# Two-layer hybrid encoder on one core: first loads in wider rows, whole conditioning sums, and group A's queries prepared by head pairs

## The chip, the cores and the metric

The kernel runs on one core of a Trainium2 chip. The metric is device time in microseconds (us), the median of several executions. The engines are named as in the profile: PE (TensorE matmul; PEld is its weight load), DVE (VectorE), ACT (ScalarE), POOL (GpSimd) and SP (SyncE, which issues the DMAs here).

## What is computed

One batch of 1024 tokens of width 1024 goes through two layers and a final RMSNorm, all in float32.

```
mod = silu(c) @ ada_w[layer] + ada_b[layer]; shift, scale, gate = split(mod, 3)
h = rms_norm(x, norm_w[layer]) * (1 + scale) + shift
layer 0: qa, ka, va, ga, cq, ckv, kr, gb = split(h @ w_in)
         A: qa, ka = axial_rope(rms_norm(qa)), axial_rope(rms_norm(ka))   # 8 heads of 64, 2 key heads
            oa = softmax(qa ka^T / 8) va * silu(ga)
         B: latent attention from cq, ckv, kr (8 heads), * silu(gb)
         y = concat(oa, ob) @ w_out
layer 1: windowed attention with 16 heads, * silu(gate), @ w_out
x = x + gate * y        (each layer);   out = rms_norm(x)
```

The change touches three things in layer 0: the shift and scale sums of the conditioning, the normalisation of the first 512 tokens, and the per-head normalisation and rotation of group A's queries and keys.

## The kernel before

The engine calls of the program aren't issued where they stand. A `Recorder` (whose one emitting line, L483, is the line of nearly all rows of the profile) collects every operation with its dependences, a priority (its place in the program, plus a shift) and a cost, runs a list schedule over the engines, PSUM banks and SBUF buffers, and then writes out a fixed order for each engine. The function `cost` prices a two-input operation on POOL at 147 ns plus 2.11 ns for each element of a partition. On the chip each engine works through its own list in order and waits at an instruction whose operands aren't there. So a change in a function moves instructions on all engines, and the place that an instruction got in the list holds also where its operands come later than planned.

Matrix products are split into high and low parts: a factor is rounded to fp32r (`h`), the rest is kept (`l`), and three products (`mm3`) make one exact one. The stages that matter here:

- **Start.** `xT_half(0)` loads x of the first 512 tokens, transposed, in eight chunks `kc` of 128 features, squares them on ACT, adds them on DVE, and `rstd_rows` turns the sums into 1/rms (transposes on PE, two reductions on DVE, a power on POOL, four transposes on PE). `warm` puts idle transposes into PE's list here, 14 of them and then 20. DVE multiplies all eight chunks by 1/rms. Then for each `kc`: `ada_mods` makes the scale and shift column (a weighted row sum of 1024 columns each, `ada_sum`, in two parts of 512 columns, and one addition), ACT applies them twice (`modulate`, way "normed": the fp32r `hT00h` and the float32 value), DVE subtracts (`hT00l`), and PE takes that chunk into the products `c1` (keys, values and latents) and `c3` (queries) of four token tiles: 24 matmuls for each chunk.
- **The rest of the projections.** `c2` (compressed queries) of the first half, the same for the second 512 tokens (`hT01`), then `c1`, `c3` and `c2` of its four tiles.
- **Keys and queries of group A.** The keys of all 1024 tokens lie in `karaw`; they are normalised and rotated by key head, and then transposed and split into `khh` (ACT) and `kll` (DVE), which every score product of group A reads. The queries are handled by token tile in `q_rope_a(i)`: all eight heads of 128 tokens at once, eight times; ACT squares, DVE reduces, POOL makes the power, DVE multiplies, POOL and DVE rotate, POOL adds. Each tile is written to `q_sp` in HBM. `q_stack_a(p)` later loads the two heads of pair p for all tokens (pair 0 comes from SBUF), transposes them on PE and splits them into `Qa`.
- **Attention of group A.** 16 groups (head, half of the queries). For each of four query tiles `softmax_unit` makes scores on PE, a maximum on DVE, an exponential on ACT (`Pa`), a reciprocal on DVE, and POOL scales `Pa`. `pv_step` transposes the four on PE, splits them (`hla`) and multiplies with the values `VA`. Between them `gate_fill` puts the matmuls of the gates (`wg0`, `wg4`, ...).

Of the kernel before, what the change touches and what calls it, by code (L numbers as in the profile page):

```python
# [505 lines left out]
def encoder_kernel(ctx: ExitStack, tc: tile.TileContext, xt, ada_t, w_c1, w_c2, w_c3, w_g0, w_uq, w_ukv, w_out0, w_v1,  # L506
# [130 lines left out]
    def ada_sum(o, src, scale, first, name, mark, parts):  # L637

        s = U(name)
        load(s, src, mark)  # L640
        n = 1024 // parts
# [5 lines left out]
    def ada_mods(l, kc, mark=None):  # L647

        t = SM(f"ada{l}{kc}")
        k = 8 * l + kc  # L650
        for j in range(2):
            o = [t[:, 2 * q + j:2 * q + j + 1] for q in range(2)]
            scale, first = (0.5, cols[:, C_BSH + k:C_BSH + k + 1]) if j else (nwh[:, k:k + 1], a0[:, k:k + 1])
            ada_sum(o, ada_t[l * 24 + 8 * (1 - j) + kc], scale, first, f"ada{l}{kc}{j}", mark, 2)
        nc.vector.tensor_tensor(out=mods[:, 2 * k:2 * k + 2], in0=t[:, 0:2], in1=t[:, 2:4], op=ALU.add)

    def ada_gate(l, b, mark=None):
        for t in range(4 * b, 4 * b + 4):
            k = 8 * l + t
            ada_sum([gcol[:, k:k + 1]], ada_t[l * 24 + 16 + t], 0.25, g0[:, k:k + 1], f"adag{l}{t}", mark, 1)  # L660
# [17 lines left out]
    def rstd_rows(accs, name):  # L678
# [20 lines left out]
        nc.gpsimd.tensor_tensor(out=r[:, 0:nt], in0=v, in1=mhalf[:, 0:nt], op=ALU.pow)  # L699
# [70 lines left out]
    xT = {}  # L770

# [29 lines left out]
    marks = {}  # L801
# [24 lines left out]
    qz = [U(f"qz{j}").rearrange("p (t c) -> p t c", t=2) for j in range(4)]  # L826
# [11 lines left out]
    def c3_end(i):  # L838
        nc.scalar.copy(qz[i // 2][:, i % 2, :], c3[i])
# [35 lines left out]
    with issue_after(m_):  # L875
        for i in range(E3, 4):
            c3_part(i, w3, range(KC))
            c3_end(i)
        for i in range(C2_EARLY):
            c2_tile(i)  # L880
    for i in range(E1, NT):
        c1_part(i, w1, range(KC))
        c1_end(i)
# [959 lines left out]
```

## Time and profile before

| | us |
|---|---|
| median of 3 runs | 1205.65 (1204.23 to 1207.63) |
| the profiled execution, its own time | 1205.73 |
| its span, first to last instruction | 1204.0 |
| PE busy | 1168.4 (97%) |
| PEld busy | 986.9 (82%) |
| DVE busy | 920.2 (76%) |
| ACT busy | 658.4 (55%) |
| POOL busy | 557.0 (46%) |

The profiled execution stands 0.08 us above the median. Its span leaves 1.73 us of its own time outside. Busy shares are means over the whole span; rows of the trace give the start of an instruction in us from the span's start and then its length. A bracket at a row's end is the time for which the engine stood idle before it, and what it waited for.

### The profile page before, as it was taken

The page shows a single profiled execution, that of the slowest core. Times are in us where ns is not written, and L with a number is a line of the kernel's source. Part 1 is how long each engine was busy: PE and PEld are TensorE (multiplying, and loading weights), DVE is VectorE, ACT ScalarE, POOL GpSimd, SP SyncE. Part 2 cuts the span into 40 slices and gives each one's busy share as a digit, 9 for nine tenths or more (in the row PEclk, how much of TensorE's full clock was granted, in tenths as well). Part 3 has the DMA queues.
Part 4 walks back from the last instruction along what each step waited for, and adds up shares of the span by engine and source line. Part 5 has one row for each costly group of instructions (what it writes and reads, how often), then busy time and mean ns, then how long its engine had stood idle before and what let it go on. Part 6 is the DMA issues. An engine that isn't in the chain of part 4 may idle for free.

```text
span 1204.0 us, 17922 instructions
## 1 busy us (share of the span) xinstructions
PE 1168.4 (97%) x6320; PEld 986.9 (82%) x6320; DVE 920.2 (76%) x1787; ACT 658.4 (55%) x1346; POOL 557.0 (46%) x551
## 2 busy tenths in 40 slices
PE   6999899999999999999999999999999999999996
PEld 6898778787778878788878888988888888888896
DVE  7976587878687988888798995749886697788343
ACT  4643256666665777787787312228755556653212
POOL 0057765435564655444447233305465265467321
PEclk9999899999999999999999999999999999999999
DMA  9601123120121121001025584200011121045112
GB/s 351 258 1 58 37 103 123 36 105 19 50 95 53 59 82 54 22 15 45 8 73 217 202 314 142 86 1 13 25 53 54 52 88 54 19 180 189 69 71 71
DMA packets 37338, 106.72 MB, mean 89 GB/s; under 512 B 3840, under 2 KB 9472, under 8 KB 37248
## 3 DMA queue, kind: packets, MB, share of 16 engines
q1 hardware_dynamic: 36480, 103.48, 23.9%
q0 software_dynamic: 768, 2.10, 0.7%
q8 instruction: 49, 0.80, 0.3%
q14 instruction: 41, 0.34, 0.1%
HBM read 82.36 MB, written 23.20 MB: 88 GB/s over the span
## 4 chain that ended last, share of the span: by engine, by line
PE 83%; DVE 9%; ACT 4%; issue 2%; DMA 1%; POOL 0%; SPq 0%; POOLq 0%; DVEq 0%; ACTq 0%
PE psum L483 83%; DVE nm L483 2%; DVE hla L483 1%; DVE p L483 1%; ACT q L483 1%; ACT k L483 1%; DVE Qa L483 1%; DMA ada<-in_ada_t 1%; ACT Pa L483 0%; DVE ada L483 0%; DVE q L483 0%; ACT p L483 0%; DVE hl L483 0%; ACT hlb L483 0%; DVE hlb L483 0%
## 5 line engine op out<-in xcount | busy, mean ns | idle before, releaser
L483 DVE TENSOR_REDUCE nm<-psum 128x1 f32<-128x1024 f32 x128 | 155.4, 1217 | 19.0 <-PE psum L483 17.4
L483 POOL TENSOR_SCALAR p<-p,dn 128x384 f32<-128x384 f32 (+1 forms) x128 | 74.1, 597 | 160.3 <-DVE dn L483 79.3
L483 DVE TENSOR_TENSOR hla<-psum,hla 128x512 fp32r<-128x512 f32 x128 | 84.9, 682 | 25.0 <-ACT hla L483 24.4
L483 PE MATMUL psum<-hla,VA 128*128 128x512 f32 x256 | 94.4, 421 | 5.4 <-DVE hla L483 4.0
L483 ACT CAST hla<-psum 128x512 fp32r<-128x512 f32 x128 | 72.4, 592 | 43.4 <-PE psum L483 36.4
L483 PE MATMUL psum<-ident,Pa 128*128 128x128 f32 x512 | 93.8, 272 | 0.8 <-DVE q L483 0.8
L483 POOL TENSOR_SCALAR Pb<-Pb,rs 128x1024 f32<-128x1024 f32 x64 | 71.8, 1125 | 45.6 <-DVE rs L483 43.9
L483 PE MATMUL psum<-hlb,VB 128*128 128x512 f32 x256 | 90.8, 427 | 2.1 <-DVE hlb L483 1.4
L483 POOL TENSOR_SCALAR Pa<-Pa,rs 128x1024 f32<-128x1024 f32 x64 | 76.5, 1198 | 34.7 <-DVE rs L483 32.0
L483 ACT ACTIVATE Pa<-psum,nm 128x1024 f32<-128x1024 f32 x64 | 71.5, 1118 | 32.1 <-DVE nm L483 24.6
L483 DVE TENSOR_TENSOR hlb<-psum,hlb 128x512 fp32r<-128x512 f32 x128 | 82.3, 683 | 7.7 <-ACT hlb L483 7.0
L483 ACT ACTIVATE Pb<-psum,nm 128x1024 f32<-128x1024 f32 x64 | 71.8, 1123 | 25.2 <-DVE nm L483 22.2
L483 PE MATMUL psum<-k,q 128*128 128x512 f32 x256 | 84.1, 400 | 0.2 <-ACT Pb L483 0.2
L483 DVE CUSTOM_DVE_ANT_0 p<-psum,bias,rows_g 128x384 f32<-128x384 f32 (+1 forms) x128 | 70.5, 579 | 12.7 <-PE psum L483 11.5
L483 PE MATMUL psum<-ident,Pb 128*128 128x128 f32 x512 | 79.4, 272 | 0.0
L483 ACT ACTIVATE p<-p,nm 128x384 f32<-128x384 f32 (+1 forms) x128 | 74.1, 585 | 7.1 <-DVE nm L483 7.1
L483 PEld LDWEIGHTS psum<-ident,Pa 128*128 128x128 f32 x512 | 65.0, 140 | 12.4 <-DVE q L483 1.0
L483 ACT CAST hlb<-psum 128x512 fp32r<-128x512 f32 x128 | 68.9, 602 | 9.1 <-PE psum L483 7.8
L483 ACT COPY ot<-psum 64x512 f32<-64x512 f32 x64 | 37.4, 584 | 65.8 <-PE psum L483 65.3
L483 PEld LDWEIGHTS psum<-ident,Pb 128*128 128x128 f32 x512 | 63.2, 140 | 11.3
L483 POOL TENSOR_TENSOR sq<-sq,sq 128x256 f32<-128x256 f32 (+2 forms) x22 | 26.2, 1190 | 76.8 <-ACT sq L483 76.6
L483 PE MATMUL psum<-oTl,wo1h 128*128 128x256 f32 (+1 forms) x192 | 61.2, 320 | 0.0
(748 smaller groups left out, 3653.3 us busy)
## 6 DMA issues: line engine op xcount, KB each, us to landing
ada<-in_ada_t SPq DMA_DIRECT2D x32, 512.0 KB, 8.3
adag<-in_ada_t SPq DMA_DIRECT2D x16, 512.0 KB, 4.8
o<-spill SPq DMA_DIRECT2D x12, 512.0 KB, 6.6
wo0s<-in_w_out SPq DMA_DIRECT2D x8, 512.0 KB, 8.7
xr<-in_xt SPq DMA_DIRECT2D x8, 512.0 KB, 10.0
x_sp<-xr SPq DMA_DIRECT2D x8, 512.0 KB, 3.0
wo1s<-in_w_out SPq DMA_DIRECT2D x8, 512.0 KB, 5.6
x1r<-x_sp SPq DMA_DIRECT2D x8, 512.0 KB, 5.3
```

Of the source, the lines that this page charges most:

```text
L483: fn(*[real(v) for v in a], **{k: real(v) for k, v in kw.items()})
```

## The change

- The first 512 tokens are loaded in four DMAs of 128 x 1024 (4 KB for each partition) in place of eight of 128 x 512.
- `ada_sum` makes one sum of 1024 columns and writes it into `mods` directly; the two halves and their addition go. The sums of layer 0 are ordered behind the power of `rstd_rows`.
- The multiplication by 1/rms is made chunk by chunk, in the loop that uses the chunk. The first reads PSUM, the others a copy in SBUF that ACT makes once.
- `c3_end` copies the four head pairs of a tile into four buffers `qz[p]` (128 tokens x 128 columns each), so ACT makes four copies of 128 columns in place of one of 512.
- `norm_rope_a` replaces the key code and `q_rope_a`. It handles one pair (or the keys) for one half of the tokens. Keys and pair 0 of the first half come right after the first half's projections, the second half after `c3`. Pairs 1 to 3 are written to `q_sp` raw and are normalised and rotated when `q_stack_a` has loaded them, in the attention of group A, with `eng` = POOL for what DVE did.

```
-    def ada_sum(o, src, scale, first, name, mark, parts):
+    def ada_sum(o, src, scale, first, name, mark, late=None):
-        for q in range(parts):
-            c = slice(q * n, (q + 1) * n)
-            nc.vector.tensor_tensor_reduce(out=s[:, c], in0=s[:, c], in1=cb[:, c], scale=scale,
-                                           scalar=0.0 if q else first, op0=ALU.mult, op1=ALU.add, accum_out=o[q])
+        behind(nc.vector.tensor_tensor_reduce(out=s, in0=s, in1=cb, scale=scale, scalar=first, op0=ALU.mult,
+                                              op1=ALU.add, accum_out=o), late)
...
-            for kc in range(KC):
-                load(chunk(xT[0], kc), xt[0, kc // 2][:, (kc % 2) * 512:(kc % 2 + 1) * 512])
+            for k2 in range(4):
+                load(xT[0][k2], xt[0, k2])
...
     def c3_end(i):
-        nc.scalar.copy(qz[i // 2][:, i % 2, :], c3[i])
+        for p in range(4):
+            nc.scalar.copy(qz[p][:, i, :], c3[i][:, p * P:(p + 1) * P])
...
     for kc in range(KC):
+        ada_mods(0, kc, late=marks["rstd", "x0"])
         c = chunk(xT[0], kc)
-        nc.vector.tensor_tensor(out=c, in0=c, in1=rp0, op=ALU.mult)
-    for kc in range(KC):
-        ada_mods(0, kc)
+        nc.vector.tensor_tensor(out=c, in0=c, in1=rb0 if kc else rp0, op=ALU.mult)
+        if kc == 0:
+            rb0 = rows_copy(rp0, "x0")
...
+    def norm_rope_a(x, tab, name, half, eng):
+        w = U(f"nr{name}{half}")
+        h4 = slice(4 * half, 4 * half + 4)
+        t1_ = w[:, 0:512].rearrange("p (t c) -> p t c", t=4)
+        t2_ = w[:, 512:1024].rearrange("p (t c) -> p t c", t=4)
+        x = x[:, h4, :]
+        nc.scalar.activation(t1_, x, AF.Square)
+        ss = SM(f"ss{name}")
+        nc.vector.tensor_reduce(out=ss[:, 0:8].rearrange("p (t g) -> p t g", t=4),
+                                in_=t1_.rearrange("p t (g d) -> p t g d", g=2), axis=AX.X, op=ALU.add)
+        r = rstd_of(ss[:, 0:8], HD, 8)
+        x4 = x.rearrange("p t (g d) -> p t g d", g=2)
+        eng.tensor_tensor(out=x4, in0=x4, op=ALU.mult, in1=r[:, 0:8].rearrange("p (t g) -> p t g", t=4)
+                          .unsqueeze(3).broadcast_to([P, 4, 2, 64]))
+        for g in range(2):
+            x_ = x[:, :, g * 64:(g + 1) * 64]
+            nc.gpsimd.tensor_tensor(out=t1_[:, :, g * 64:(g + 1) * 64], in0=x_, in1=tab[0][:, h4], op=ALU.mult)
...
+            for s in range(2):
+                eng.tensor_tensor(out=t5[:, :, :, s, :], in0=x5[:, :, :, 1 - s, :], in1=tab[1][:, h4, :, s, :], op=ALU.mult)
+        nc.gpsimd.tensor_tensor(out=x, in0=t1_, in1=t2_, op=ALU.add)
...
+    k_stack_a(0)
+    norm_rope_a(qz[0], qtab, "q0", 0, nc.vector)
...
+    k_stack_a(1)
+
+    norm_rope_a(qz[0], qtab, "q0", 1, nc.vector)
+    q_sp = dr.tile([3, P, 1024], F32, name="q_sp")
+    for p in range(1, 4):
+        nc.sync.dma_start(out=q_sp[p - 1], in_=qz[p].rearrange("p t c -> p (t c)"))
...
         if p:
+            s = U(f"qp{p}")
+            load(s, q_sp[p - 1], mark)
+            s = s.rearrange("p (t c) -> p t c", t=8)
+            for half in range(2):
+                norm_rope_a(s, qtab, f"q{p}", half, nc.gpsimd)
         else:
+            s = qz[0]
```

How the lists of the engines change at the places that the prediction speaks of:

**DVE at the start.** `ISA ada` is a conditioning sum, `ss` the norm's chain, `xT` times `psum` (or `rbx`) the multiplication by 1/rms, `hT00l` the low part of a chunk. Rows that repeat a kind are left out here. Before:

```order
L483 TENSOR_REDUCE ss<-psum 128x4 x2
L483 ISA ada_130,ada_129<-ada_130,cb,nwh 128x512
L483 TENSOR_SCALAR ss<-ss 128x4
L483 ISA ada_131,ada_129<-ada_131,cb,cols 128x512
L483 SCALAR_TENSOR_TENSOR ss<-ss 128x4
L483 TENSOR_TENSOR xT_115<-xT_115,psum 128x512 x2
L483 TENSOR_TENSOR xT_116<-xT_116,psum 128x512 x2
L483 TENSOR_TENSOR xT_117<-xT_117,psum 128x512 x2
L483 TENSOR_TENSOR xT_118<-xT_118,psum 128x512 x2
L483 TENSOR_TENSOR w30l_137<-w30s_135,w30h_136 128x1024
L483 TENSOR_TENSOR hT00l_92<-xT_115,hT00h_88 128x512
```

Now, in the same place:

```order
L483 TENSOR_REDUCE ss<-psum 128x4 x2
L483 TENSOR_SCALAR ss<-ss 128x4
L483 SCALAR_TENSOR_TENSOR ss<-ss 128x4
L483 ISA ada_129,mods<-ada_129,cb,a_85,nwh 128x1024
L483 ISA ada_130,mods<-ada_130,cb,cols 128x1024
L483 TENSOR_TENSOR xT_115<-xT_115,psum 128x512
L483 TENSOR_TENSOR w10l_134<-w10s_132,w10h_133 128x832
L483 TENSOR_TENSOR w30l_137<-w30s_135,w30h_136 128x1024
L483 TENSOR_TENSOR hT00l_92<-xT_115,hT00h_88 128x512
```

The norm's chain no longer has sums between its steps, and one multiplication stands ahead of the first `hT00l` in place of eight.

**PE behind the last `c2` of the second half.** `ident,karaw` and `ident,qz` are the transposes of keys and pair 0; `hT..,wg0` are gate matmuls; `khh,Qa` is the first score product. Before (the 44 remaining matmuls of that gate stand behind the last row):

```order
L483 MATMUL psum<-ident,karaw 128x128 x8
L483 MATMUL psum<-w2h_178,hT01l_101 128x256
L483 MATMUL psum<-ident,qz_109 128x128 x2
L483 MATMUL psum<-ident,qz_110 128x128 x2
L483 MATMUL psum<-ident,qz_111 128x128 x2
L483 MATMUL psum<-hT00h_88,wg0h_282 128x512
L483 MATMUL psum<-hT00l_92,wg0h_282 128x512
L483 MATMUL psum<-hT01h_96,wg0h_282 128x512
L483 MATMUL psum<-hT01l_100,wg0h_282 128x512
L483 MATMUL psum<-khh_208,Qa_278 128x512
```

Now (between the last two rows here stand the other gate matmuls and the eight transposes of `ckvraw`):

```order
L483 MATMUL psum<-ident,qz_109 128x128 x4
L483 MATMUL psum<-hT00h_88,wg0h_251 128x512
L483 MATMUL psum<-hT00l_92,wg0h_251 128x512
L483 MATMUL psum<-hT00h_88,wg0l_252 128x512
L483 MATMUL psum<-ident,qz_109 128x128 x4
L483 MATMUL psum<-ident,cqraw_113 128x128 x3
L483 MATMUL psum<-khh_192,Qa_247 128x512
```

The keys' eight transposes have moved ahead of `c2` of the second half (four into its `c1`, four behind its `c3`), and all 48 matmuls of the gate now stand ahead of the first score product.

**POOL in the attention of group A.** `Pa` scaled by `rs` is a softmax tile; `nrq` and `qp` are pair 1 being normalised and rotated. Before, this stretch holds only softmax tiles, gate weights and gate products. Now:

```order
L483 TENSOR_SCALAR Pa_297<-Pa_297,rs 128x1024
L483 TENSOR_TENSOR qp_304<-qp_304,r 128x512
L483 TENSOR_SCALAR v<-ssq_310 128x8
L483 TENSOR_TENSOR nrq_305<-qp_304,qtab 128x4x64
L483 TENSOR_TENSOR nrq_305<-qp_304,qtab 128x4x2x16
L483 TENSOR_TENSOR r<-v,mhalf 128x8
L483 TENSOR_TENSOR qp_304<-qp_304,r 128x512
L483 TENSOR_TENSOR nrq_309<-qp_304,qtab 128x4x64
L483 TENSOR_TENSOR qp_304<-nrq_305 128x512
L483 TENSOR_SCALAR Pa_322<-Pa_322,rs 128x1024
```

Rows that repeat a kind are left out. In all, twelve POOL instructions of pair 1, and one product with a gate, stand between the last softmax tile of one group and the first of the next; the others of the pair follow between later tiles.

## Rows read from the trace of the kernel before

**Rows 1.** The page, busy time of the engines: us, share of span, instructions.

```profile
PE 1168.4 (97%) x6320; PEld 986.9 (82%) x6320; DVE 920.2 (76%) x1787; ACT 658.4 (55%) x1346; POOL 557.0 (46%) x551
```

**Rows 2.** The page, chain that ended last: shares of the span by engine.

```profile
PE 83%; DVE 9%; ACT 4%; issue 2%; DMA 1%; POOL 0%; SPq 0%; POOLq 0%; DVEq 0%; ACTq 0%
```

**Rows 3.** Stretches of the start: length, busy us of each engine, clock, DMA share, GB/s.

```profile
9.00:10.00 1.00, 0.00 (x0) 0.00 (x0) 1.00 (x2) 0.95 (x2) 0.00 (x0) 1.00 0.94 350
...
12.00:14.00 2.00, 2.00 (x20) 2.00 (x19) 1.78 (x5) 0.00 (x0) 0.00 (x0) 1.00 1.02 416
```

**Rows 4.** Timeline, the norm of the first half and PE's first matmul.

```profile
10.96 0.63 ACT L483 ACTIVATE sq<-xT 128x512 f32<-128x512 f32 x1 [0.22 <-DMA xT<-in_xt]
...
13.15 1.28 DVE L483 TENSOR_REDUCE ss<-psum 128x4 f32<-128x512 f32 x2
...
16.00 1.41 POOL L483 TENSOR_TENSOR r<-ss,mhalf 128x4 f32<-128x4 f32 x1 [12.93 <-DVE ss L483]
...
17.47 1.11 PE L483 MATMUL psum<-ident,r 128*128 128x128 f32 x4 [3.19 <-POOL r L483]
...
21.59 0.44 PE L483 MATMUL psum<-w10h,hT00h 128*128 128x416 f32 x1
```

**Rows 5.** Timeline and one stretch: the multiplications, PE's wait for the second chunk, the clock.

```profile
18.61 4.87 DVE L483 TENSOR_TENSOR xT<-xT,psum 128x512 f32<-128x512 f32 x8 [0.95 <-PE psum L483]
...
29.62 0.46 PE L483 MATMUL psum<-w10h,hT00h 128*128 128x416 f32 x1 [2.05 <-ACT hT00h L483]
...
32.00:34.00 2.00, 2.00 (x7) 1.74 (x7) 2.00 (x3) 1.89 (x3) 0.00 (x0) 0.50 1.03 411
```

**Rows 6.** Timeline of PE, the last chunk of the first half and its end.

```profile
61.20 0.35 PE L483 MATMUL psum<-w13h,hT00h 128*128 128x416 f32 x1
...
63.48 0.39 PE L483 MATMUL psum<-w33h,hT00h 128*128 128x512 f32 x1
...
66.20 0.60 PE L483 MATMUL psum<-ident,sq 128*128 128x128 f32 x4
```

**Rows 7.** Conditioning sums on DVE: timeline, two chunks' first parts; then tile adag.

```profile
25.14 0.80 DVE L483 CUSTOM_DVE_ANT_0 ada<-ada,cb,a 128x512 f32<-128x512 f32 x1
...
27.83 0.80 DVE L483 CUSTOM_DVE_ANT_0 ada<-ada,cb,a 128x512 f32<-128x512 f32 x1
...
L483 DVE CUSTOM_DVE_ANT_0 adag<-adag,cb,g x16: 1248/1273/1918, 220.0 to 989.4; 128x1024 f32<-128x1024 f32 x16
```

**Rows 8.** Timeline of PE at the first score product; then tile khh, ns min/median/max.

```profile
132.85 0.50 PE L483 MATMUL psum<-hT00h,wg0h 128*128 128x512 f32 x1 [1.07 <-POOL wg0h L483]
...
134.06 0.50 PE L483 MATMUL psum<-hT01h,wg0h 128*128 128x512 f32 x1 [0.47 <-DVE kll L483]
...
137.59 0.79 PE L483 MATMUL psum<-khh,Qa 128*128 128x512 f32 x1 [2.80 <-DVE Qa L483]
...
143.30 0.60 PE L483 MATMUL psum<-hT00h,wg0l 128*128 128x512 f32 x1
...
L483 ACT CAST khh<-psum x8: 577/580/584, 128.8 to 133.0; 64x512 fp32r<-64x512 f32 x8
L483 DVE TENSOR_TENSOR kll<-psum,khh x8: 681/688/694, 131.2 to 136.1; 64x512 fp32r<-64x512 f32 x8
```

**Rows 9.** POOL: shapes from 60 to 160 us (busy us, mean ns); timeline; attention by stretches.

```profile
L483 POOL TENSOR_TENSOR r<-v,mhalf 128x8 f32<-128x8 f32 x11 | 18.2, 1657 | 0.6
L483 POOL TENSOR_TENSOR qt<-qz,qtab 128x512 f32<-128x512 f32 x8 | 11.4, 1425 | 8.9 <-DVE qz L483 8.9
...
L483 POOL TENSOR_TENSOR ktab<-tabs,rows_g 128x256 f32<-128x256 f32 x2 | 2.3, 1186 | 0.0
...
232.49 1.29 POOL L483 TENSOR_TENSOR og('0', 0)_331<-og('0', 0)_331,gT 64x512 f32<-64x512 f32 x1 [9.40 <-DVE og('0', 0)_331 L483]
...
200.00:300.00 100.00, 99.34 (x522) 79.79 (x521) 80.91 (x126) 60.80 (x108) 46.90 (x36) 1.00 0.22 74
300.00:400.00 100.00, 98.57 (x535) 79.81 (x534) 76.60 (x117) 60.64 (x112) 54.72 (x51) 1.00 0.21 70
```

More of the change, by code (lines that the diff above doesn't have):

```diff
@@ L698, in rstd_rows @@
         r = SM("r")
-        nc.gpsimd.tensor_tensor(out=r[:, 0:nt], in0=v, in1=mhalf[:, 0:nt], op=ALU.pow)
+        marks["rstd", name] = nc.gpsimd.tensor_tensor(out=r[:, 0:nt], in0=v, in1=mhalf[:, 0:nt], op=ALU.pow)
         pr = PA(f"rb{name}")
@@ L770, in encoder_kernel @@
     xT = {}
+    marks = {}
     def chunk(t, kc):
@@ L824, in c1_end @@
         sub(VA[i // 4][:, i % 4, :, 1, :], v3, f(hi))
-    qz = [U(f"qz{j}").rearrange("p (t c) -> p t c", t=2) for j in range(4)]
+    qz = [U(f"qz{p}").rearrange("p (t c) -> p t c", t=8) for p in range(4)]
     c3 = {}
@@ L874, in encoder_kernel @@
         modulate(0, kc, chunk(xT[1], kc), rb0, hT0[1][kc], MOD_WAY[0][kc % len(MOD_WAY[0])])
[L875 to L883, printed above, removed]
-    for i in range(4, NT):
-        c3_part(i, w3, range(KC))
-        c3_end(i)
-    kr_sp = dr.tile([P, 256], F32, name="kr_sp")
-    nc.sync.dma_start(out=kr_sp, in_=krraw[:, 0:256])
     rows_g = const.tile([P, 144], F32, name="rows_g")
@@ L935, in encoder_kernel, with k_stack_a @@
+        nc.gpsimd.tensor_tensor(out=x, in0=t1_, in1=t2_, op=ALU.add)
     khh = [UR(f"khh{g}") for g in range(2)]
     kll = [UR(f"kll{g}") for g in range(2)]
-    for half in range(2):
+    def k_stack_a(half):
+        norm_rope_a(karaw, ktab, "k", half, nc.vector)
         pt = PT(f"kaT{half}")
@@ L951, in encoder_kernel @@
             sub(kll[g][q, c], pt[r, :], f(khh[g][q, c]))
-    def q_rope_a(i):
-        q = qz[i // 2][:, i % 2, :]
-        q3 = q.rearrange("p (h d) -> p h d", h=8)
-        tw = U(f"qt{i}")
-        t1, t2 = tw[:, 0:512], tw[:, 512:1024]
-        nc.scalar.activation(t1, q, AF.Square)
-        ss = SM("ssq")
-        nc.vector.tensor_reduce(out=ss[:, 0:8], in_=t1.rearrange("p (h d) -> p h d", h=8), axis=AX.X, op=ALU.add)
-        r = rstd_of(ss[:, 0:8], HD, 8)
-        nc.vector.tensor_tensor(out=q3, in0=q3, in1=r[:, 0:8].unsqueeze(2).broadcast_to([P, 8, 64]), op=ALU.mult)
-        nc.gpsimd.tensor_tensor(out=t1.rearrange("p (h d) -> p h d", h=8), in0=q3,
-                                in1=qtab[0][:, i, :].unsqueeze(1).broadcast_to([P, 8, 64]), op=ALU.mult)
-        q5 = q.rearrange("p (h b s e) -> p h b s e", h=8, b=2, s=2)
-        t5 = t2.rearrange("p (h b s e) -> p h b s e", h=8, b=2, s=2)
-        for s in range(2):
-            nc.vector.tensor_tensor(out=t5[:, :, :, s, :], in0=q5[:, :, :, 1 - s, :],
-                                    in1=qtab[1][:, i, :, s, :].unsqueeze(1).broadcast_to([P, 8, 2, 16]), op=ALU.mult)
-        nc.gpsimd.tensor_tensor(out=q, in0=t1, in1=t2, op=ALU.add)
-    q_sp = dr.tile([T, 512], F32, name="q_sp")
-    for i in range(NT):
-        q_rope_a(i)
-        nc.sync.dma_start(out=q_sp[i * P:(i + 1) * P, :], in_=qz[i // 2][:, i % 2, :])
+    k_stack_a(0)
+    norm_rope_a(qz[0], qtab, "q0", 0, nc.vector)
+    with issue_after(m_):
+        for i in range(E3, 4):
+            c3_part(i, w3, range(KC))
+            c3_end(i)
+        for i in range(C2_EARLY):
+            c2_tile(i)
+    for i in range(E1, NT):
+        c1_part(i, w1, range(KC))
+        c1_end(i)
+    for i in range(4, NT):
+        c3_part(i, w3, range(KC))
+        c3_end(i)
+    kr_sp = dr.tile([P, 256], F32, name="kr_sp")
+    nc.sync.dma_start(out=kr_sp, in_=krraw[:, 0:256])
+    k_stack_a(1)
[3 more added lines that the diff above has]
+        nc.sync.dma_start(out=q_sp[p - 1], in_=qz[p].rearrange("p t c -> p (t c)"))
     for i in range(C2_EARLY, NT):
```

38 lines of the change are left out of this document (8 added, 30 removed).

## The prediction

> **What bounds the kernel now.** I read first the busy line: PE works 97% of the span, the next engine 76% [rows 1]. Then the chain of waits: 83% of it is PE, 9% DVE, 4% ACT, 1% DMA [rows 2]. So the time is TensorE's, and its matmul work is the same after the change. A gain can come from two things alone: stretches in which PE waits, and stretches in which it runs at the lower of its two clock levels (1.2 and not 2.4 GHz). Third, the timeline of PE, to find these stretches near the change. There are three: everything before the first matmul at 21.59 us [rows 4], the eight chunks of the first half from there to 66.20 [rows 5, 6], and the stall at the first score product of group A at 137.59 [rows 8]. In the attention behind it PE is busy 98.57 to 99.34% [rows 9], so there is next to nothing to win there, and something to lose.
>
> The sum is made against the profiled execution, 1205.73 us, which is 0.08 above the median of the runs; its last part outside the span (1.73) is taken as unchanged. A measurement of this kernel can tell about 0.3% from no change, here 3.6 us.
>
> **A. The way to the first matmul: -2.2 us (0 to -3.5).** It leads over the last square of x, the reductions, the power, four transposes [rows 4], the multiplication and the first chunk.
> - Loads. In a stretch where only 2 KB rows of x come in, 350 GB/s arrive; where 4 KB rows come, 416 [rows 3]. The half is 2.1 MB: 6.0 us by the one, 5.05 by the other, so up to 0.95 earlier. Against that the last DMA now brings two chunks, and ACT squares them one after the other: +0.63 [rows 4]. Net -0.3. Bounds: +0.6 (rate unchanged) and -0.95.
> - Conditioning sums. Before, sums of 512 columns stand between DVE's steps of the norm; one is 0.80 long as the trace has it [rows 7], of which I count 0.65 as delay, since waits between the steps hide the rest. Two stand between the reductions at 13.15 and the power at 16.00, and one ahead of the second reduction [rows 4]: 3 x 0.65 = -1.9. They now stand behind the power, and cost PE nothing as long as the first one or two end while POOL and PE make 1/rms (16.00 to 18.61 [rows 4, 5], 2.6 us, against 2 x 1.27 [rows 7]).
>
> The Trainium skill, "DMA: Bandwidth & Descriptors", section Specifications, puts the full rate at 512 bytes for a transfer and above. By that rule 2 KB and 4 KB rows are alike and the end would be 0.95 us later, 1196.3; the two stretches of this trace (350 and 416 GB/s) speak against it.
>
> **B. The chunks of the first half: -3.3 us (0 to -4.6).** One chunk is 12 matmuls of `c1` (61.20 to 63.48: 2.28) and 12 of `c3` (63.48 to 66.20: 2.72), 5.0 us at full clock [rows 6]; eight are 40.0. They took 66.20 - 21.59 = 44.6. The 4.6 too many are a wait of 2.05 ahead of the second chunk and a stretch at clock 0.50 behind it [rows 5]. The cause stands on DVE: eight multiplications, 4.87 us in one piece, before the first `hT00l` [rows 5]. Now one stands there (4.87 / 8 = 0.61), so the inputs of the second chunk come up to 4.3 us earlier, more than the wait. Whether DVE then keeps pace: a chunk's conditioning took 2.69 (25.14 to 27.83), and is now two sums of 1.27 = 2.55 [rows 7]; with one multiplication (0.61), the subtraction (one more of 128 x 512 from two sources, 0.61) and two low parts of weights every second chunk (832 and 1024 columns, by the sums' 1.27 for 1024 about 2.3, 1.15 a chunk), DVE needs some 4.9 for each chunk and PE 5.0. That is close, so I leave 1.3 of the 4.6 in place. Lower bound 0: DVE or the loads set the pace and PE waits as long, in other places. ACT's added copy of 1/rms stands beside the first chunk's matmuls; if it were late, chunk two would be, by about one ACT pass (0.63 [rows 4]), inside that remainder.
>
> **C. The stall at the first score product: -7.1 us (0 to -7.2).** Before, PE waits 1.07, 0.47 and 2.80 there, 4.34 in all, and the 14 matmuls from 137.59 to 143.30 take 5.7 us, 0.41 each, where a full-clock one of 512 columns takes 0.227 [rows 6, 8]: some 2.8 lost to the clock behind the waits. Keys of all tokens (`khh` 4 + 4 x 0.58, `kll` 4 + 4 x 0.69 [rows 8]) and tile after tile of queries stand in that chain. Now the first half of the tokens is done beside the second half's projections, and behind the last `c3` are left, from the four transposes of keys on (0.6): DVE's four `kll` behind the first `khh` (0.58 + 4 x 0.69 = 3.3 [rows 8]), the queries' reduction (0.64 [rows 4]), the power (1.66 at most) with its small step (0.3, an estimate), a multiplication (0.61 [rows 5]), POOL's two products (1.19 each at most) and its sum (1.43 [rows 9]); together 10.9. PE meanwhile has 96 matmuls of `c2` (256 columns, half of 0.227: 10.9), four transposes of `qz` (0.6 [rows 6]) and six of the gate's matmuls (1.4) until it wants the second token half: 12.9. The margin is 2 us there. Behind it stand the other 42 matmuls of the gate (9.5), which cover the splits into `Qa`. If a cover went, each us past it would be a wait again; the next to be late would be `Qa` of the second token half.
>
> The keys' steps move past `c2` on PE, ACT and DVE; eight transposes of PE change place, not number. `c3_end` makes four ACT copies for one, 24 more in all for the eight tiles; ACT is at 55% [rows 1], and a copy of less than the 0.58 of a `khh` [rows 8] delays at most the release of one PSUM bank: nothing, at most 0.6 x 3 = 1.8 on the last tile, about C's margin. SP issues three stores of `q_sp` in place of eight; the raw pairs are ready as soon as `c3` is done, so nothing queues behind a rotation there any more. Pair 1's load now stands behind a store of the latents; it is wanted only in the attention.
>
> **D. Pairs 1 to 3 beside the attention: +2.2 us (0 to +11.4).** For each pair and token half POOL now does: a small step and a power (1.66 each at most), a product and a sum of 512 (1.43), two rotations of 256, and four of 128. The nearest row for those with a stride has 1.19 for 256 [rows 9]; a plain one can be no less than half of 1.43. So 7.4 to 9.3 us for each block, six blocks, 44 to 56 us of POOL where it was 47 to 55% busy [rows 9]. The list was made with 147 + 2.11 ns per element: 7.4. So up to 1.9 us a block can come late against the list, 6 x 1.9 = 11.4. What absorbs it: POOL stands idle up to 9.40 us within one group [rows 9], and gate matmuls stand between the score products and PE's use of a softmax tile. I take a wait of about 0.75 a pair, the size of the small waits seen (0.47 to 1.07 [rows 8]), three times. A gain is excluded: PE had 98.57 to 99.34% there [rows 9].
>
> **Sum:** 1205.7 - 2.2 - 3.3 - 7.1 + 2.2 = 1195.3.
>
> **Rivals.**
> - *A new wait takes the place of the removed one (0.12).* Pair 0's second token half comes later than PE's transposes of it, and the gate's matmuls, which stand behind these in PE's fixed order, wait too. For it: a chain over three engines with 2 us of margin. Against: the 10.9 us of `c2` cover its start. Then only A, B and D count: 1205.7 - 5.5 + 2.2 = 1202.4 at worst, 1200.2 without D.
> - *The start stays paced (0.14).* Loads or DVE set the step of the chunks, so that an earlier norm only waits longer later. For it: 411 GB/s with a full DMA share where PE is at half clock [rows 5], and 4.9 against 5.0 on DVE. Then C and D count: 1205.7 - 7.1 + 2.2 = 1200.8.
> - *Slower: POOL becomes the bound in group A (0.14).* One mechanism: softmax tiles queue behind pair blocks in POOL's fixed order, and PE waits for `Pa` and for the transposes of `qp`. Price: up to 56 us, if nothing of a block hides. For it: 12 pair instructions stand in one piece ahead of a group's first softmax tile, about 12 us, against a hole of 9.40. It decides from 12.6 / 6 = 2.1 us of PE wait a block, where A to C are eaten up; with 4 us a block, 1205.7 - 12.6 + 24 = 1217.
>
> The Trainium skill, "GPSIMD Engine Reference", section 4.1, gives elementwise work to VectorE and expects about half its pace from GpSimd. By it alone a block would cost about twice what DVE needed; no run here yet shows both on one shape.
>
> **How the numbers follow.** The forecast, with all four terms near their sizes, has 0.60 and its own range 1190.5 (A and B at their bounds, C 7.1, D 0: 1205.7 - 8.1 - 7.1) to 1200. The two middle rivals (0.26) lie at 1200.2 to 1202.4, so the range goes from 1189.5, one us lower for the spread of a median, to 1203.0, and leaves out most of the third. Faster by over 0.3% means below 1202.0: forecast 0.60, start paced 0.13, new wait 0.08, a mild third rival 0.02, together 0.83. Slower means above 1209.3: 0.09 of the third rival. Within: 0.08.
>
> **What would show it.** A: first matmul near 19.4. B: no wait at the second chunk, clock 1.00 throughout, first half's end near 61. C: no idle of PE over 0.5 us and no half clock between the last `c2` and the first score product. D: POOL's share in the 200 to 400 us up by 15 to 20 points, with PE's at least at 98%. Wrong would be: waits of PE for `Pa` or `qp` that add up to over 5 us, for POOL's chain at `qz`, or a DVE that falls behind PE chunk by chunk.

## The result and the profile after

The changed kernel took 1194.91 us (median of five runs, 1192.36 to 1198.82) where the kernel before took 1205.65 (1204.23 to 1207.78) in the same session: a ratio of 0.9909, 95% interval 0.9884 to 0.9935, or 10.7 us less. The forecast was 1195.3. The profiled execution is the fastest of the five, 1192.36, with a span of 1190.6; what follows is read from it, so its terms add up to 13.2 and not 10.7 us.

The busy line of the page [rows 1]: PE's share rises by one point, its busy time falls by 6.5 us. Its matmuls are the same in number and kind, so those 6.5 are matmuls at a faster pitch, and the rest of the gain is waits.

```profile
PE 1161.9 (98%) x6320; PEld 982.7 (83%) x6320; DVE 904.8 (76%) x1693; ACT 657.1 (55%) x1371; POOL 581.1 (49%) x591
```

To see where the time went, I gave every PE instruction of both traces its pitch at full clock (0.227 us for 512 columns, 0.19 for 416, 0.17 for 384, 0.12 for 256, 0.11 for a transpose), added them up in the order of the trace (the work sum), and compared the starts of the instructions at which equal sums were reached. What is left of a difference is wait or clock; where the orders differ, it is good to about half a us.

| PE work done | place | before | after | difference |
|---|---|---|---|---|
| 49.5 | end of the first half | 66.2 | 59.3 | -6.9 |
| 114 | last products ahead of the stall | 130.6 | 124.5 | -6.1 |
| 125 | behind the stall | 149.7 | 135.6 | -14.1 |
| 160 | attention of A, early | 188.3 | 171.6 | -16.7 |
| 400 | behind group A | 445.1 | 431.9 | -13.2 |
| all | last matmul | 1197.1 | 1183.9 | -13.2 |

So the change has three gains and one loss: start 6.1 (6.9, of which 0.8 is given back by 114), stall 8.0 and 2.6 right behind it, and 3.5 lost in the attention of group A.

**Start.** The timeline of the changed kernel: the last four squares of x on ACT, the power on POOL, PE's transposes of its result, its first matmul, its last of the first half, and its first wait behind that.

```profile
7.76 2.43 ACT L483 ACTIVATE sq<-xT 128x512 f32<-128x512 f32 x4
...
13.41 2.12 POOL L483 TENSOR_TENSOR r<-ss,mhalf 128x4 f32<-128x4 f32 x1 [10.34 <-DVE ss L483]
...
15.59 0.65 PE L483 MATMUL psum<-ident,r 128*128 128x128 f32 x4 [1.47 <-POOL r L483]
...
18.35 0.46 PE L483 MATMUL psum<-w10h,hT00h 128*128 128x416 f32 x1
...
59.04 0.39 PE L483 MATMUL psum<-w33h,hT00l 128*128 128x512 f32 x1
...
68.28 0.65 PE L483 MATMUL psum<-ident,r 128*128 128x128 f32 x4 [0.40 <-POOL r L483]
```

The last square ends at 10.19 (11.59 [rows 4]), the power starts at 13.41 (16.00), the first matmul at 18.35 (21.59), and the first half ends at 59.04 + 0.23 = 59.27 (66.20 [rows 6]). The wait of 2.05 at the second chunk [rows 5] is gone. The eight chunks take 40.9 us, against 44.6 before and 40.0 at full clock. PE does not wait right ahead of its first matmul, before or after: it does the 20 idle transposes of `warm` there. Of the 3.2 us at the first matmul 1.9 come with the transposes of `r` (17.47 [rows 4] to 15.59); the other 1.3 stand in the idle transposes, a part of which ran at the lower clock before (17.45 to 20.87 us).

**Stall.** Of the waits at the first score product [rows 8] none is left; the nearest of PE behind it is 0.17. Before, two more waits stood behind the stall, at the transposes of the latents. Here are first those two of the kernel before with the splitting of the first gate's weights on POOL (`wg0h`, `wg0l`), and then the same places after.

```profile
131.75 1.05 POOL L483 TENSOR_SCALAR wg0h<-wg0s 128x1024 fp32r<-128x1024 f32 x1
...
133.16 2.36 POOL L483 TENSOR_TENSOR wg0l<-wg0s,wg0h 128x1024 fp32r<-128x1024 f32 x1
...
163.78 0.66 PE L483 MATMUL psum<-ident,cqraw 128*128 128x128 f32 x4 [1.19 <-DVE gT L483]
...
165.58 0.66 PE L483 MATMUL psum<-ident,cqraw 128*128 128x128 f32 x4 [0.37 <-DVE cqT L483]
```

```profile
103.63 2.04 POOL L483 TENSOR_SCALAR wg0h<-wg0s 128x1024 fp32r<-128x1024 f32 x1
105.75 2.40 POOL L483 TENSOR_TENSOR wg0l<-wg0s,wg0h 128x1024 fp32r<-128x1024 f32 x1
...
137.90 0.48 PE L483 MATMUL psum<-khh,Qa 128*128 128x512 f32 x1
...
143.62 0.47 PE L483 MATMUL psum<-hT00h,wg4h 128*128 128x512 f32 x1 [0.17 <-DVE cqT L483]
```

The weights of the first gate are ready 27 us earlier: POOL no longer has eight tiles of queries ahead of them. The first score product starts at the same time as before (137.90 and 137.59), but with 44 more matmuls of the gate already done.

**Attention.** Two new waits stand at the changes to pairs 2 and 3, each put down to an exponential of ACT (`Pa`), which reads the PSUM buffer that the next scores want. Behind the second, PE runs at the lower clock for 3.4 us (322.04 to 325.45), which costs about half of that, 1.7. The rows are PE's timeline, three stretches (columns as in [rows 3]) and the POOL operations of pairs 1 to 3 (ns min/median/max).

```profile
251.93 0.50 PE L483 MATMUL psum<-khh,Qa 128*128 128x512 f32 x1 [1.91 <-ACT Pa L483]
...
321.51 0.50 PE L483 MATMUL psum<-khh,Qa 128*128 128x512 f32 x1 [1.88 <-ACT Pa L483]
...
200.00:300.00 100.00, 97.83 (x519) 79.46 (x518) 80.60 (x127) 60.16 (x110) 77.96 (x76) 1.00 0.19 64
300.00:400.00 100.00, 97.25 (x543) 80.14 (x542) 79.92 (x130) 62.00 (x118) 54.79 (x56) 0.98 0.19 60
322.00:325.00 3.00, 3.00 (x9) 2.35 (x8) 2.13 (x4) 1.50 (x4) 3.00 (x3) 0.51 0.00 0
...
L483 POOL TENSOR_TENSOR nrq<-qp,qtab x36: 448/470/1452, 160.8 to 298.3; 128x128 f32<-128x128 f32 x24, 128x256 f32<-128x256 f32 x12
...
L483 POOL TENSOR_TENSOR qp<-qp,r x6: 1035/1054/1282, 159.3 to 283.4; 128x512 f32<-128x512 f32 x6
```

PE's share in these stretches was 99.34 and 98.57 before [rows 9]. POOL's rises from 46.90 to 77.96% in the first, and not at all in the second, where no pair is turned any more.

### The profile page after: what moved, and what is told of

The parts are those of the page before. It is cut to its first block, busy times and chain, and to the rows that moved or that the text cites. A ratio compares the mean times of both kernels' runs of the same rounds, so it can differ in the third digit from the quotient of the medians.

```text
span 1190.6 us, 17868 instructions
## 1 busy us (share of the span) xinstructions
PE 1161.9 (98%) x6320; PEld 982.7 (83%) x6320; DVE 904.8 (76%) x1693; ACT 657.1 (55%) x1371; POOL 581.1 (49%) x591
## 4 chain that ended last, share of the span: by engine, by line
PE 84%; DVE 6%; ACT 4%; DMA 3%; issue 1%; POOL 1%; SPq 0%; POOLq 0%; DVEq 0%; ACTq 0%
PE psum L483 84%; DVE nm L483 2%; DMA ada<-in_ada_t 2%; DVE p L483 1%; DMA w2s<-in_w_c 1%; DMA w31s<-in_w_c 1%; ACT k L483 1%; ACT q L483 1%; ACT Pa L483 0%; DVE hla L483 0%; ACT p L483 0%; DVE hl L483 0%; DVE q L483 0%; DVE hlb L483 0%; POOL r L483 0%
## 5 line engine op out<-in xcount | busy, mean ns | idle before, releaser
L483 POOL TENSOR_SCALAR Pa<-Pa,rs 128x1024 f32<-128x1024 f32 x64 | 73.6, 1154 | 39.2 <-DVE rs L483 37.0
```

The costliest lines, as they stand in the source:

```text
L483: fn(*[real(v) for v in a], **{k: real(v) for k, v in kw.items()})
```

## The experiments

**The start alone.** The loads, sums and loop of the change on the kernel before; `norm_rope_a` and the buffers by pairs are left out.

```
-            for kc in range(KC):
-                load(chunk(xT[0], kc), xt[0, kc // 2][:, (kc % 2) * 512:(kc % 2 + 1) * 512])
+            for k2 in range(4):
+                load(xT[0][k2], xt[0, k2])
...
+        ada_mods(0, kc, late=marks["rstd", "x0"])
+        nc.vector.tensor_tensor(out=c, in0=c, in1=rb0 if kc else rp0, op=ALU.mult)
```

> The kernel before with the start of the change alone (4 KB loads, single sums behind the power, multiplication chunk by chunk); keys and queries of group A as before. Theory (three separate PE stretches): the first half ends near 59.5 us in place of 66.20, the waits at the first score product (4.3 us) and behind it stay, so 1205.65 - 7 = 1198.7, between 1197 and 1201. Rival (the stall is set by something that does not start with the first half, so an earlier start only lengthens it): the waits around the first score product grow by 3 us or more, and the time is above 1201.5.

Measured 1198.95 us, ratio 0.9944 (0.9927 to 0.9962); the first half ends at 59.6, and PE's waits around the first score product are as they were:

```profile
126.20 0.50 PE L483 MATMUL psum<-hT00h,wg0h 128*128 128x512 f32 x1 [1.12 <-POOL wg0h L483]
127.36 0.50 PE L483 MATMUL psum<-hT01h,wg0h 128*128 128x512 f32 x1 [0.42 <-DVE kll L483]
130.90 0.80 PE L483 MATMUL psum<-khh,Qa 128*128 128x512 f32 x1 [2.81 <-DVE Qa L483]
```

1.12, 0.42 and 2.81 against 1.07, 0.47 and 2.80 [rows 8], all 6.7 us earlier. The start's gain arrives whole at the end.

**The preparation alone.** The changed kernel with the three start pieces taken back to the old code.

```
-            for k2 in range(4):
-                load(xT[0][k2], xt[0, k2])
+            for kc in range(KC):
+                load(chunk(xT[0], kc), xt[0, kc // 2][:, (kc % 2) * 512:(kc % 2 + 1) * 512])
...
-        ada_mods(0, kc, late=marks["rstd", "x0"])
+        nc.vector.tensor_tensor(out=c, in0=c, in1=rp0, op=ALU.mult)
```

> The changed kernel with the start of before (2 KB loads, half sums inside the norm, eight multiplications ahead); only the new preparation of group A's keys and queries is left of the change. Theory: the first half ends near 66.2 again, no wait over 0.5 us at the first score product, the attention gives about 3.5 us back: 1205.65 - 10.5 + 3.5 = 1198.6, between 1196.5 and 1201. Rival (the earlier start is what makes the keys' and queries' chain fit): waits of PE of 2 us or more between the last c2 and the first score product, and above 1201.5.

Measured 1199.18 us, ratio 0.9951 (0.9934 to 0.9968). No wait over 0.5 us is left between `c2` and the first score product; the two waits in the attention stand there with 1.92 and 1.89. The medians of the two kernels with half the change each fall by 6.8 and 6.5 us from the 1205.7 of their session; together that is 13.3, where the whole change has 10.7 by its median and 13.2 by its profiled execution. The pieces add up within the scatter of the runs.

**Pairs turned by DVE.** One word of `q_stack_a`.

```
-                norm_rope_a(s, qtab, f"q{p}", half, nc.gpsimd)
+                norm_rope_a(s, qtab, f"q{p}", half, nc.vector)
```

> The changed kernel with pairs 1 to 3 multiplied and rotated by DVE in place of POOL inside the attention (POOL keeps the power, two products and the sum). Theory P (the two PE waits of 1.9 us for Pa at the changes to pairs 2 and 3 come from POOL's longer blocks): both waits fall under 0.5, POOL's share in the 200 to 300 us falls by some 10 points, 2 to 5 us faster than the change, 1190 to 1193. Theory L (they come from where the lists put the splits into Qa beside maxima and low parts on DVE and ACT, whoever rotates): two waits of 1.5 us or more remain there and the time is within 2 us of the change or above it.

Measured 1199.49 us: by the medians 4.6 slower than the change. Its trace is of the fastest of seven executions (1195.23); between the work sums 160 and 400 it loses 6.1 us on the kernel before, the change 3.5. POOL's share in 200 to 300 us falls to 67, DVE's rises to 90, and both waits stay. The rows are PE's waits, the stretch, and the same rotation on either engine.

```profile
253.77 0.50 PE L483 MATMUL psum<-khh,Qa 128*128 128x512 f32 x1 [1.94 <-ACT Pa L483]
...
298.89 0.50 PE L483 MATMUL psum<-hla,VA 128*128 128x512 f32 x1 [1.17 <-DVE hla L483]
...
325.79 0.50 PE L483 MATMUL psum<-khh,Qa 128*128 128x512 f32 x1 [1.89 <-ACT Pa L483]
...
200.00:300.00 100.00, 95.15 (x499) 76.02 (x497) 90.34 (x143) 59.01 (x108) 67.03 (x55) 1.00 0.19 64
...
L483 DVE TENSOR_TENSOR nrq<-qp,qtab x24: 261/292/2469, 163.5 to 303.3; 128x128 f32<-128x128 f32 x24
```

So POOL's slower pace in the rotations isn't what PE waits for. DVE does one such rotation in 0.29 us, POOL in 0.47, and yet PE loses more with DVE, which makes the maxima and low parts of the attention too: a wait of 1.17 for `hla` from DVE has come. The Trainium skill ("GPSIMD Engine Reference", section 4.1) gives elementwise work to VectorE and expects about half of VectorE's pace from GpSimd. On this shape the pace is 1.6 to 1, and the move to VectorE cost time, with DVE at 90% of the stretch.

**Pairs before the attention.**

```
-            for half in range(2):
-                norm_rope_a(s, qtab, f"q{p}", half, nc.gpsimd)
...
     for p in range(1, 4):
+        for half in range(2):
+            norm_rope_a(qz[p], qtab, f"q{p}", half, nc.vector)
         nc.sync.dma_start(out=q_sp[p - 1], in_=qz[p].rearrange("p t c -> p (t c)"))
```

> The changed kernel with pairs 1 to 3 normalised and rotated before the attention, by token halves and with DVE as pair 0 is, and stored rotated; the attention only loads, transposes and splits them, as before. Theory P: POOL's pair blocks are gone from the attention, the two 1.9 us waits with them, 2 to 5 us faster there; at the first score product no wait over 1 us as long as pair 0 keeps its place in the lists. Theory L: the waits at the changes to pairs 2 and 3 stay. Rival to both: the six blocks queue ahead of pair 0 or of the gate's weights on POOL (about 40 us of POOL between 60 and 150 us), a stall of 2 to 7 us returns before the first score product, and the time is 1196 to 1202.

Measured 1195.90 us. The two waits of the attention vanish (between the work sums 160 and 400 this kernel gains 2.1 us on the kernel before, where the change loses 3.5), so theory L as written falls: the same splits stand there. But between 125 and 160 it loses 5.5 us on the kernel before, just behind the first score product: it waits there for exponentials, with 6.8 us at the lower clock behind the second wait and no gate matmuls at hand, since the second gate's weights are split on POOL at 143 to 147 us here and at 129 to 133 in the change:

```profile
142.66 0.50 PE L483 MATMUL psum<-khh,Qa 128*128 128x512 f32 x1 [1.16 <-ACT Pa L483]
...
145.53 0.80 PE L483 MATMUL psum<-khh,Qa 128*128 128x512 f32 x1 [1.68 <-ACT Pa L483]
```

**Pairs one group earlier.** Theory M was formed after these runs: the pair is ready so late in its group that the lists place PE's transposes of it behind the last gate matmuls.

```
-            if n % 4 == 2 and n < 12:
-                q_stack_a(n // 4 + 1, mark_of(n - 2))
+            if n % 4 == 1 and n < 12:
+                q_turn_a(n // 4 + 1, mark_of(n - 2))
+            if n % 4 == 2 and n < 12:
+                q_stack_a(n // 4 + 1)
```

> The changed kernel with load, normalisation and rotation of pairs 1 to 3 one group of the attention earlier (still on POOL), transposes and splits of the pair in the group where they are. Theory M (the rotation makes the pair ready so late in its group that the lists put PE's transposes and the splits into Qa behind the last gate matmuls of that group, and nothing is left to fill the wait for Pa): the lists now have the last gate matmul 10 entries ahead of the transposes of pair 2 (28 in the change), both 1.9 us waits fall under 0.5, the half clock behind the second goes, and the time falls by 3 to 5 us: 1190 to 1192.5. Theory P (POOL's added 45 us itself makes softmax tiles late): POOL's share stays, the waits come back elsewhere, within 1.5 us of the change.

Measured 1191.10 us (1190.58 to 1191.89), ratio 0.9877 (0.9863 to 0.9892): faster than the kernel before. All four executions lie below all five of the change (1192.36 to 1198.82), but the intervals of the two ratios just overlap; trace against trace it is 2.0 us ahead of the change. Both waits and the half clock are gone, with POOL still at 74%; a smaller wait of 1.30 has come in pair 1's groups:

```profile
222.93 0.50 PE L483 MATMUL psum<-hla,VA 128*128 128x512 f32 x1 [1.30 <-DVE hla L483]
...
200.00:300.00 100.00, 97.67 (x516) 78.69 (x516) 81.18 (x126) 60.82 (x110) 73.64 (x68) 1.00 0.22 74
300.00:400.00 100.00, 98.27 (x556) 80.98 (x555) 82.29 (x134) 63.83 (x120) 56.13 (x56) 1.00 0.19 60
```

Between the work sums 160 and 400 it loses 0.9 us on the kernel before, the change 3.5, of which about 1.7 is the half clock. Theory P falls, and theory M holds with a condition more: 29 entries of PE's list stand between the last gate matmul and the pair's transposes at all three pairs of the change (10 here), and pair 1 shows no wait. There the next gate's matmuls (`wg1`) stand ahead of the score product that would wait, and so they do at pair 2 in this kernel (`wg2`, ahead of the score product at 254.48); in the change `wg2` comes behind it. PE's timeline, two rows of the change and one of this kernel:

```profile
180.31 0.48 PE L483 MATMUL psum<-hT00h,wg1h 128*128 128x512 f32 x1
...
254.78 0.39 PE L483 MATMUL psum<-hT00h,wg2h 128*128 128x512 f32 x1
```

```profile
252.28 0.40 PE L483 MATMUL psum<-hT00h,wg2h 128*128 128x512 f32 x1
```

**First token half late.**

```
-    k_stack_a(0)
-    norm_rope_a(qz[0], qtab, "q0", 0, nc.vector)
     with issue_after(m_):
...
+    k_stack_a(0)
+    norm_rope_a(qz[0], qtab, "q0", 0, nc.vector)
     k_stack_a(1)
```

> The changed kernel with the first token half of keys and of pair 0 prepared behind c3, together with the second half, in place of beside the second half's projections; all else as changed. Theory (the margin of the chain at the first score product is some 2 us and the early first half is what gives it): DVE, ACT and POOL have about 8 us more between c3 and the first score product; PE waits there by 3 to 8 us in all, with a stretch at half clock, 1198 to 1204. Rival (the 48 gate matmuls moved ahead of the first score product are what removed the stall, about 11 us of cover): no wait over 1 us before the first score product, and the time within 2 us of the change.

Measured 1193.32 us, within the runs of the change; no wait ahead of the first score product. The move in the text moved less in the lists: the first half's reductions still start at 64 us, and only the keys' transposes and splits went behind `c3`. The second token half of pair 0 is transposed at 132.58 (126.68 in the change), and PE has gate matmuls for that time. So the run tests a late second half of pair 0 and late keys, not a late normalisation of the first half.

```profile
111.77 1.03 PE L483 MATMUL psum<-ident,karaw 128*128 128x128 f32 x8
...
132.58 0.60 PE L483 MATMUL psum<-ident,qz 128*128 128x128 f32 x4
```

**All multiplications ahead**, and **half sums**, each on the changed kernel:

```
     for kc in range(KC):
-        ada_mods(0, kc, late=marks["rstd", "x0"])
         c = chunk(xT[0], kc)
-        nc.vector.tensor_tensor(out=c, in0=c, in1=rb0 if kc else rp0, op=ALU.mult)
+        nc.vector.tensor_tensor(out=c, in0=c, in1=rp0, op=ALU.mult)
+    for kc in range(KC):
+        ada_mods(0, kc, late=marks["rstd", "x0"])
```

> The changed kernel with all eight multiplications by 1/rms ahead of the chunks, as before (from PSUM, no copy of 1/rms); loads and sums as changed. Theory (B): the second chunk waits again some 2 us with a stretch at half clock behind it, the first half ends 2 to 4 us later than in the change (61 to 63.5), 1196.5 to 1199. Rival (half sums and their additions were DVE's burden in the chunks, not the order): no wait over 0.7 us at the second chunk, the first half's end within 1 us of the change, 59 to 60.3.

```
-        behind(nc.vector.tensor_tensor_reduce(out=s, in0=s, in1=cb, scale=scale, scalar=first, op0=ALU.mult,
-                                              op1=ALU.add, accum_out=o), late)
+        n = 1024 // parts
+        for q in range(parts):
+            c = slice(q * n, (q + 1) * n)
+            nc.vector.tensor_tensor_reduce(out=s[:, c], in0=s[:, c], in1=cb[:, c], scale=scale,
+                                           scalar=0.0 if q else first, op0=ALU.mult, op1=ALU.add, accum_out=o[q])
...
+        nc.vector.tensor_tensor(out=mods[:, 2 * k:2 * k + 2], in0=t[:, 0:2], in1=t[:, 2:4], op=ALU.add)
```

> The changed kernel with the conditioning sums in two parts of 512 and an addition again, free to stand between the steps of the norm as before; loads and multiplications as changed. Theory (A): the power starts 1.5 to 2 us later than in the change after the last square, the first half ends 1.5 to 2.5 us later, 1196 to 1198. Rival (the first matmul came earlier by the loads alone): power and first half's end within 0.7 us of the change, 1194 to 1196.

With the multiplications ahead 1201.36 us: the wait that was expected at the second chunk comes ahead of the first matmul, 5.09 us, a stretch of four us at the lower clock follows, and the first half ends at 65.1. With half sums 1199.97 us: the power starts at 15.10 (13.41 in the change) and the first half ends at 63.4. PE's and POOL's timeline, the first row of the former kernel, the others of the latter:

```profile
23.16 0.72 PE L483 MATMUL psum<-w10h,hT00h 128*128 128x416 f32 x1 [5.09 <-ACT hT00h L483]
```

```profile
15.10 1.74 POOL L483 TENSOR_TENSOR r<-ss,mhalf 128x4 f32<-128x4 f32 x1 [11.98 <-DVE ss L483]
...
17.81 4.47 PE L483 MATMUL psum<-ident 128*128 128x128 f32 x20
21.94 0.69 PE L483 MATMUL psum<-w10h,hT00h 128*128 128x416 f32 x1
...
63.17 0.39 PE L483 MATMUL psum<-w33h,hT00l 128*128 128x512 f32 x1
```

Both are directions as expected, and both are larger: 5.8 and 4.1 us at the first half's end, most of it at the first matmul already (23.16 and 21.94; 18.35 in the change). In the former DVE makes eight multiplications and the sums ahead of the first chunk. In the latter the idle transposes ran at the lower clock (0.50 from 17 to 22 us), so a part of its 4.1 is clock, and no run separates it. Together the two are more than the start's whole gain of 7, so they are not independent terms.

**Gates first, on the kernel before**, and the same together with the start:

```
-        return wload([w_g0[ft]], P, f"wg{ft}", mark=mark, lo_eng="pool")
+        with rec.at(shift=-200 if ft in (0, 4) else 0):
+            return wload([w_g0[ft]], P, f"wg{ft}", mark=mark, lo_eng="pool")
```

> The kernel before, with one thing changed: the two instructions that split the weights of gates 0 and 4 on POOL get an earlier priority, so that they stand ahead of the last products of the queries there; start, keys, queries and attention as before. The lists then have all 48 matmuls of gate 0 ahead of the first score product (4 before). Theory G (the stall was PE without gate matmuls, because their weights queued behind eight tiles of queries on POOL): the waits at the first score product (4.3 us) and the half clock behind them are gone or under 1 us, 1205.6 - 7 to -10 = 1195.5 to 1198.5, with keys and queries still prepared by tiles. Theory K (the recorded one: the chain of keys and queries is too long): the waits stay at 3 us or more, between the gate matmuls and the first score product, and the time is above 1202.

> The start of the change and the earlier split of the gate weights together, on the kernel before; the new preparation of group A is left out. Theory G: start (-6.5) and stall (-7 to -10) add up, and the attention gives nothing back: 1189 to 1192, faster than the change. Theory K: as the start alone, 1197 to 1200.

Measured 1203.27 us, ratio 0.9976 (0.9961 to 0.9991), and 1197.28 us, ratio 0.9928 (0.9916 to 0.9941). The first trace is of the slowest of its ten executions (1207.85). In it the stall at the first score product is gone, 7.3 us by the work sum 125; by 160 all of it is lost again, at the transposes of the latents, whose normalisation on DVE now comes late:

```profile
155.83 0.44 PE L483 MATMUL psum<-ident,ckvraw 128*128 128x128 f32 x2 [3.11 <-DVE ckvraw L483]
...
166.40 0.66 PE L483 MATMUL psum<-ident,cqraw 128*128 128x128 f32 x4 [1.40 <-DVE cqT L483]
```

With the start it is the same, 14.7 us gained by 130 less 6 that are lost by 150, in waits of 1.77 and 2.28 for `Pa` from POOL and the lower clock behind them. Theory G is right on the stall, and wrong on the time, which is what theory K gave for both kernels: the order alone mostly moves the wait. By the medians it is worth 3.0 us on the kernel before (1206.3 in that session), where 7 to 10 were expected.

**Loads of 2 KB** on the changed kernel:

```
-            for k2 in range(4):
-                load(xT[0][k2], xt[0, k2])
+            for kc in range(KC):
+                load(chunk(xT[0], kc), xt[0, kc // 2][:, (kc % 2) * 512:(kc % 2 + 1) * 512])
```

> The changed kernel with the first tokens loaded in eight DMAs of 2 KB rows again; all else as changed. Theory (rows of 4 KB are faster, and more than the second square costs): the last square of x ends 0.7 to 1.5 us later than in the looks at 4 KB rows (9.9 to 10.3 us), the first half ends 0.5 to 1.5 us later than 59.3. Rival (the rate is the same and only a DMA more is issued): the last square ends at 9.5 to 10.2 us, the first half at 59 to 59.5.

Measured 1196.49 us, within the runs of the change. In the trace the last square ends at 11.15 (10.19), the first half at 59.95 (59.27):

```profile
7.86 3.29 ACT L483 ACTIVATE sq<-xT 128x512 f32<-128x512 f32 x5 [0.49 <-DMA xT<-in_xt]
...
59.72 0.39 PE L483 MATMUL psum<-w33h,hT00l 128*128 128x512 f32 x1
```

About 1 us at the squares and 0.7 at the first half's end go with the rows' width, or with the smaller number of DMAs; no run separates the two. Here is the stretch from 5 to 8 us, in which x arrives, of the kernel before, the change, and this kernel (columns as in [rows 3]); its packets are of 2 KB, 4 KB and 2 KB, with 4-byte ones beside them.

```profile
5.00:8.00 3.00, 3.00 (x20) 3.00 (x18) 0.69 (x1) 1.17 (x2) 0.00 (x0) 1.00 0.97 313
5.00:8.00 3.00, 2.65 (x25) 2.41 (x23) 1.52 (x3) 2.54 (x5) 0.00 (x0) 1.00 1.02 419
5.00:8.00 3.00, 2.76 (x26) 2.52 (x24) 1.29 (x2) 1.38 (x3) 0.00 (x0) 1.00 0.93 311
```

## Why the prediction was right, and where it was not

The time came within 0.4 us of the forecast, and part of that is luck. By the terms of the profiled execution the gain would have been 2.8 larger; that execution lies 2.55 below the median of its kernel. The change has one trace, so where its slower executions lose those us isn't shown; the other kernels' traces show one place where executions differ by 2.1 us whatever the change (below, under the last heading).

- **A and B, the start: forecast -5.5, measured -6.9 at the first half's end.** First matmul 3.2 us earlier (forecast 2.2), chunks 3.7 us shorter (3.3), but this split is not a property of the change: in the seven traces with the same start (the change, the start alone, pairs turned by DVE, before the attention and one group earlier, first token half late, and gates first together with the start) the first matmul lies between 17.70 and 19.36 us, and the half ends at 59.3 to 59.6 in all of them. Within A the loads were mis-sized: I counted -0.3, since the last DMA brings two squares; the squares ran without a wait for it, and their end came 1.4 us earlier here, about 1 by the run with 2 KB rows. The 350 GB/s were read from a stretch, 9 to 10 us, that already held 4 KB rows (83 packets of 2 KB and 55 of 4 KB); where x alone arrives, 313 stand against 419, so 6.7 us against 5.0 for the 2.1 MB. The Trainium skill ("DMA: Bandwidth & Descriptors", Specifications) puts the full rate at transfers of 512 bytes and more. The 311 GB/s with 2 KB rows and 419 with 4 KB rows do not agree with that, but the number of DMAs changed too. The sums' 1.9 is what the half sums brought back on the power (15.10 against 13.41 is 1.7). The power itself became longer, below.
- **C, the stall: forecast -7.1, measured -8.0 and -2.6 behind it.** (The half clock's 2.8 in that sum is 2.5 by its own rows, 5.7 less 14 times 0.227.) The step that failed is the reason, "the margin is 2 us". It did not decide: with the keys' splits late and pair 0's second half transposed 6 us later, no stall came, because the gate's matmuls filled the time. What PE lacked before was those matmuls. [rows 8] named it, as the wait of 1.07 for `wg0h`, and I read it as one of three waits and not as their cause. But the gates alone bring 3.0 us and not 7: with all eight tiles of queries still to be done, DVE and POOL are late 20 us further on. So it is the work of pairs 1 to 3 that had to leave this stretch, and the gate's cover is how its absence reaches PE. Of the 2.6, 1.56 are the waits at the latents (1.19 and 0.37), which I had not listed.
- **D, the attention: forecast +2.2, measured +3.5.** The size was near, the mechanism was not. A block costs POOL 7.6 us (power 1.66, product 1.05, sum 1.29, two rotations of 0.74, four of 0.47, a small step of 0.2), at the lower end of 7.4 to 9.3, and softmax tiles hardly queued behind it: they start 0.7 us behind their reciprocals on average, 0.5 before. PE waits twice for a buffer that an exponential frees, at two of three pairs, because the lists put the pair's transposes behind the last gate matmuls of its group and the next gate's behind the score product that waits; pair 1, with the next gate's ahead of it, has no wait. About 1.7 of the 3.5 is the half clock behind the second wait. One group of lead takes 2.6 of the 3.5 away, half clock included. The sign "PE at least at 98%" was missed: 97.83 and 97.25.
- **Rivals.** The new wait in the old one's place did not come at the first score product; it did come where the queries of all pairs were prepared ahead (some 5 to 7.5 us in three runs). The paced start came in small: chunk pitch is 5.1 us against 5.0 of PE, but a first matmul ahead of some 19.3 us brings nothing at the half's end, as the seven traces show. POOL as the bound did not come: 80% at most in any stretch of 100 us.

## What to carry to other kernels

When the engine that bounds waits for work that should merely fill, look for what is queued ahead of the filler's operands on another engine's fixed list; shortening the chain it is said to wait for may not be needed. A wait that an order removed came back further on here as long as the work itself stayed in the stretch, so look at the time at equal work some tens of us behind it. Work that was moved into a steady loop here wanted a lead of a whole group, though the engine that does it had room: place it so that what depends on it isn't last in its iteration.

## What was not expected of the hardware

- The power of the first half's norm on POOL (128 x 4) took 1.41 us before [rows 4], where DVE did short steps beside it, and 2.12 in the change, where a sum of 1024 columns runs on DVE at the same time (2.12 also in the other kernels with that sum there, 1.74 with the half sums). It costs 0.7 us of the 1.9 that the sums give back; no run took it away.
- Equal waits had unequal prices: behind PE's wait of 1.91 at 251.93 the granted clock stayed at 1.00, behind 1.88 at 321.51 it was 0.51 for three us. Seven traces have these two waits; the clock fell behind the first in one of them (first token half late) and behind the second in six, all but pairs turned by DVE. No run shows what decides it.
- One subtraction on DVE beside POOL, the same in all kernels, had two lengths. It makes the low part of an output weight at the end of group B's attention, while POOL splits others: 1.29 to 1.31 us in seven of the thirteen traces (the kernel before and the change among them), 3.33 to 3.37 in six, and in these PE waits 1.74 to 1.78 for `hlb` and is 2.1 us later at equal work from there on. Rows of the change, then of the kernel with 2 KB loads:

```profile
647.48 1.30 DVE L483 TENSOR_TENSOR wo0l<-wo0s,wo0h 128x1024 fp32r<-128x1024 f32 x1
```

```profile
648.37 3.35 DVE L483 TENSOR_TENSOR wo0l<-wo0s,wo0h 128x1024 fp32r<-128x1024 f32 x1
...
652.37 0.73 PE L483 MATMUL psum<-hlb,VB 128*128 128x512 f32 x2 [1.76 <-DVE hlb L483]
```
